# First feed-forward stage with four plain columns, weight splits held until the norm factor's chain is emitted, rotary tables on GpSimd in the second feed-forward stage

## The chip, the cores and the metric

The kernel runs on one core of one Trainium2 chip. The metric is the device time of one execution in microseconds (us); the number for a kernel is the median of several runs. Engines are named as in the profile: PE (TensorE matmuls), PEld (its weight loads), DVE (VectorE), ACT (ScalarE), POOL (GpSimd) and SP (SyncE, which issues the DMAs).

## The reference

A trunk of two layers in fp32 on 512 tokens of width 1024. Each layer is a half-step SwiGLU feed-forward (width 2816), an attention, and a second half-step feed-forward; all of them behind an RMS norm.

```python
def rms_norm(x, gain):
    y = xf * lax.rsqrt(jnp.mean(xf * xf, axis=-1, keepdims=True) + EPS)
    return (y * gain.astype(jnp.float32)).astype(x.dtype)

def swiglu(h, w_gate_up, w_down):
    gate, up = jnp.split(h @ w_gate_up, 2, axis=-1)
    return (jax.nn.silu(gate) * up) @ w_down

def rope_angles(positions):
    inv_freq = ROPE_THETA ** (-jnp.arange(0, ROT_DIM, 2, dtype=jnp.float32) / ROT_DIM)
    ang = positions.astype(jnp.float32)[..., None] * inv_freq
    return jnp.cos(ang), jnp.sin(ang)

for i in range(DEPTH):
    x = x + 0.5 * swiglu(rms_norm(x, norm_gains[i, 0]), ffn_w_gate_up[i, 0], ffn_w_down[i, 0])
    h = rms_norm(x, norm_gains[i, 1])
    # i = 0: stick-breaking attention; i = 1: sliding-window attention, which uses the rotary tables
    x = x + attention(h)
    x = x + 0.5 * swiglu(rms_norm(x, norm_gains[i, 2]), ffn_w_gate_up[i, 1], ffn_w_down[i, 1])
```

## The kernel before, in words

**Stages.** The kernel runs six stages in the order "0", "s", "1", "2", "w", "3". "0" to "3" are the feed-forwards, "s" the stick-breaking and "w" the sliding-window attention. x is kept in SBUF with features on the partitions, as eight tiles of 128x512 (`x[k]`). Each fp32 product is made of three matmuls: x and the weights are split into a high part (a rounding to fp32r) and a low part (what is left), and hi·hi, hi·lo and lo·hi are added. ACT casts the high part of a weight (L345), DVE subtracts for the low part (L350, in `_split`); the lines read L85 where an engine wrapper keeps program order.

**A feed-forward stage.** Its 22 hidden columns of 128 are made in two ways. The first three (`PLAIN`) are plain columns: two units each (gate and up), each unit eight k-tiles of three matmuls of 128x512, into one PSUM bank of 512 columns. The others are "seven" columns (`seven`, L528): a Strassen-like scheme with seven products of four k-tiles of three matmuls of 128x256. Their partial sums live in banks named a (tag "tr", two buffers), b (tag "pv", one) and c (tag "z", one). The down projection (`down`, L631) runs over groups of columns (`GROUPS`: 3, 3, 4, 4, 4, 4); its pieces for a group are put between the seven columns of the next group. A piece needs the `hs` of all columns of its group.

**The norm factor.** Matmuls run on x times the gain, not on the normed x; the factor 1/rms is multiplied in afterwards. `norm_tile` (L423) makes xh, xl and adds the squares into `acc`. `norm_rows` (L453) sums `acc` on PE (ss, tag "pv") and runs a chain of twelve dependent small DVE steps (nv, nr, nt). `norm_bcast` (L463) spreads the factor over the partitions (dg on ACT, bc on PE, `rbc`). `swiglu` (L486) multiplies gate and up by `rbc` (g and h on DVE, silu on ACT) and `keep` splits the result into `hs` (cast on ACT, rest on DVE). `sums_of_x` (L497) makes t0 to t3, the sums of x that the seven columns need.

**The plain part** (`plain`, L596). Units 0 to 2 use the banks of tag "mm" (three), unit 3 uses tag "z", units 4 and 5 tag "mm" again. So unit 4 takes the bank of unit 0, which is free when swiglu(0) has read it. In stage "0" the first three units run interleaved over the k-tiles. Behind the last k-tile of unit 1 (in stage "0" behind the fifth k-tile of unit 3) stand `norm_bcast`, `sums_of_x((2, 3))` and `swiglu(0)`, in this order.

**What sets the order.** A scheduler orders the instructions of each engine when the program is built; after that each engine works strictly in that order and waits for semaphores. PE always keeps the order of the code, DVE does in `plain` only (`self.order(True)`). `pump` (L289) loads and splits weights as far ahead as the rings allow: raw tiles (3, in feed-forwards 2 more), split slots (3 and 2 more) and half slots (2). SP issues the loads in the order of the code.

**The rotary tables** (`rope_tables`, L886). Some 45 dependent steps on 128x32 elements (an argument reduction and two Sin lookups on ACT) make cos and sin, which stage "w" uses. They are emitted in the output projection of stage "s", behind n = 3 (`project_out`, L819), and run on DVE.

Of the kernel before, what the change touches and what calls it, by code (L numbers as in the profile page):

```python
# [15 lines left out]
P = 128  # L16
# [10 lines left out]

PLAIN = 3
GROUPS = (3, 3, 4, 4, 4, 4)
MORE_RAWS, MORE_SLOTS, HALF_SLOTS = 2, 2, 2  # L30
# [104 lines left out]

def ffn_steps():

    steps = [("plain", u) for u in range(2 * PLAIN)]
    f, last = PLAIN, None
    for g, size in enumerate(GROUPS):  # L140
        ends = sum(GROUPS[: g + 1])
# [18 lines left out]
    return steps + [("down", len(GROUPS) - 1, n) for n in range(KD)]  # L160


def ffn_slots(steps):

    slots, units = [], []

    def slot(name, raws):
        if name not in slots:
            slots.append(name)
            units.extend(r for r in raws if r not in units)  # L170

    for step in steps:
        if step[0] == "plain":
            slot(step, [step])
        elif step[0] == "seven":
            _, p, f = step
            slot(*{
                1: (("A22 A11", f), [("g", f), ("u", f)]), 4: (("A22 A11", f), []), 5: (("S1 S3", f), []), 7: (("S1 S3", f), []),
                2: (("A12", f), []), 6: (("S2 S4", f), []), 3: (("S2 S4", f), []),
            }[p])  # L180
        else:
            _, g, n = step
            for i in range(n * GROUPS[g], (n + 1) * GROUPS[g]):
                slot(("d", g, i // KD), [("d", g, i // KD)])
    return slots, units


class _Trunk:
    def __init__(self, tc, pools, psum, aps):
# [10 lines left out]
        self.half_rings = []  # L200
        self.fp = self.stage = None
        self.roped = False

# [37 lines left out]
    def queue_ffn(self, st):  # L241

        steps = ffn_steps()
        slots, units = ffn_slots(steps)
        raw = {u: len(self.loads) + i for i, u in enumerate(units)}
# [12 lines left out]
        for step in steps:  # L258
# [7 lines left out]
            else:  # L266
                _, g, n = step
                tiles = [(at["d", g, i // KD], i % KD) for i in range(n * GROUPS[g], (n + 1) * GROUPS[g])]
            out.append((step, tiles))
# [19 lines left out]
    def pump(self):  # L289

        moved = True
        while moved:
# [275 lines left out]

    def ffn(self, st, steps, following, first=False):
        tc, nc = self.tc, self.nc  # L570
        with tc.tile_pool(name="ffn", bufs=1) as fp:
# [4 lines left out]
            self.cells, self.hs = {}, {}  # L576
            self.plain(steps[: 2 * PLAIN], first)
            last = len(GROUPS) - 1
            tail = [s for s in steps if s[0][:2] == ("down", last)]
            for step, tiles in steps[2 * PLAIN : len(steps) - len(tail)]:  # L580
# [15 lines left out]
    def plain(self, steps, first):  # L596

        xs = list(zip(self.xh, self.xl))
        banks, self.ts = {}, []
        units = range(2 * PLAIN)  # L600
        order = [(k, u) for u in units for k in range(KD)]
# [3 lines left out]
        rows, cast = ((1, KD - 1), (3, 4)) if first else ((0, KD - 1), (1, KD - 1))  # L605
        self.order(True)
        self.pump()
        for k, u in order:
            if u not in banks:
                banks[u] = self.psum.tile([P, T], F32, tag="z", name="gu", bufs=1) if u == UNITS else self.bank("gu")  # L610
            wh, wl, used = self.tile(*steps[u][1][k])
            self.mm3(banks[u], [((wh, wl), xs[k])], first=(k == 0), last=(k == KD - 1))
            if (u, k) == rows:
                self.norm_rows()
            self.used(*used)
# [10 lines left out]
    def down_terms(self, ps, g, tiles, at):  # L626
        f0 = sum(GROUPS[:g])
        for j, (n, i) in enumerate(tiles, at):
            self.mm3(ps, [(self.tile(n, i), self.hs[f0 + j])], first=(j == 0), last=(j == GROUPS[g] - 1))

    def down(self, n, g, tiles, following, ps=None):  # L631
        at = GROUPS[g] - 1 if ps is not None else 0
# [186 lines left out]
    def project_out(self, parts, opened, following):  # L819
        for n in range(KD):  # L820
# [3 lines left out]
            following(n)  # L824
            if n == UNITS and not self.roped:
                self.rope_tables()

# [58 lines left out]
    def rope_tables(self):  # L886
# [6 lines left out]
        with self.tc.tile_pool(name="rope", bufs=1) as rp:  # L893
            V = nc.vector

# [12 lines left out]
            part = _split_const(two_pi, 12, 3)  # L908
            q, t = tile_("q"), tile_("t")

# [4 lines left out]
            def fma(a, k, cst):  # L915
                V.scalar_tensor_tensor(a, k, cst, a, ALU.mult, ALU.add)

# [12 lines left out]
            for d, rest in digits:  # L930
                for m, piece in enumerate(_split_const(rest, 12, 3)):
                    if m == 0:
                        V.tensor_scalar(t, d, piece, None, ALU.mult)
# [280 lines left out]
def build(tc, aps, stages="0s12w3"):  # L1214
    from contextlib import ExitStack

    with ExitStack() as ctx:
# [27 lines left out]
        for i, st in enumerate(stages):  # L1245
# [5 lines left out]
            if st in "0123":  # L1251
                net.ffn(st, steps[st], following, first=(i == 0))
            else:
# [3 lines left out]
def layout(x, positions, norm_gains, ffn_w_gate_up, ffn_w_down, sb_w_in, sb_w_out,  # L1257
# [7 lines left out]
    for i in range(4):  # L1265
        units = []
        for name in ffn_slots(ffn_steps())[1]:
            if name[0] == "plain":
# [5 lines left out]
            else:  # L1274
                _, g, m = name
                f, size = sum(GROUPS[:g]), GROUPS[g]
                tiles = dn[i, :, f : f + size].reshape(KD * size, P, P)[m * KD : (m + 1) * KD]
# [33 lines left out]
```

## Time and profile before

| what | us |
|---|---|
| three runs | 1879.17, 1881.69, 1884.75 |
| median | 1881.69 |
| the profiled execution | 1884.44 |
| its span, first to last instruction | 1882.6 |
| PE busy | 1834.2 |
| DVE busy | 1500.1 |
| ACT busy | 938.1 |
| POOL busy | 170.2 |

The mean granted TensorE clock of the profiled execution is 0.985 of full speed. Rows of the trace are read so: a chain row has the start, the duration and what ran ("44.22 0.61 DVE g L85"); a timeline row has start, duration, engine, line, operation, out<-in, shapes, and in brackets the idle time before it and what ended that; a row of waits has who waited for whom, the total, how many times, and the longest. In a group of matmuls "a x12" are the twelve of one product.

### The profile page before, as it was taken

To read this page: it belongs to the slowest core of one execution; us is meant where nothing else is said; L and a number is where in the kernel's file an instruction comes from. 1 tells how busy PE (TensorE), PEld (TensorE's weight loads), DVE (VectorE), ACT (ScalarE), POOL (GpSimd) and SP (SyncE) were. 2 spreads that over 40 slices of the span, in tenths; PEclk is the share of its full clock that TensorE was granted. 3 is DMA by queue.
4 is the path that set the end of the run, shared out by engine and by line. 5 is a ranking of instruction groups with operands and counts; after the bars stand their busy time and mean duration, and the time that the engine had idled before them with its cause. 6 is when DMAs were issued, how large, how long until landed. Compare 5 with 4: busy or idle time off the path is not lost.

```text
span 1882.6 us, 29285 instructions
## 1 busy us (share of the span) xinstructions
PE 1834.2 (97%) x11730; PEld 1651.1 (88%) x11730; DVE 1500.1 (80%) x2426; ACT 938.1 (50%) x1497; POOL 170.2 (9%) x131
## 2 busy tenths in 40 slices
PE   7999999999999999999999999999999899999999
PEld 5999999878787789999988999999887788999998
DVE  8888888668886988878768888787678588888884
ACT  6444444465664644444446444444356564444441
POOL 1000000333230100000010000000242210000000
PEclk8999999999999999999999999999989899999999
DMA  4333333221121423333323323322211043233331
GB/s 168 101 101 101 101 104 99 69 78 57 57 68 34 134 83 98 105 109 97 106 68 123 101 90 105 119 88 92 73 58 33 12 134 101 95 108 101 102 101 57
DMA packets 48809, 170.95 MB, mean 91 GB/s; under 512 B 5792, under 2 KB 6048, under 8 KB 48672
## 3 DMA queue, kind: packets, MB, share of 16 engines
q1 hardware_dynamic: 48672, 169.07, 28.2%
q8 instruction: 92, 1.51, 0.3%
q14 instruction: 45, 0.37, 0.1%
HBM read 166.96 MB, written 2.10 MB: 90 GB/s over the span
## 4 chain that ended last, share of the span: by engine, by line
PE 80%; DVE 11%; ACT 4%; issue 3%; POOL 1%; DMA 0%; SPq 0%; ACTq 0%; DVEq 0%; POOLq 0%
PE dn L85 25%; PE a L85 23%; PE c L85 11%; PE b L85 6%; PE gu L85 4%; PE tok L85 3%; PE op L85 3%; DVE keep L732 2%; PE pv L85 1%; DVE beta L733 1%; DVE t L85 1%; DVE qs L645 1%; PE sc L85 1%; DVE wt L755 1%; ACT keep L726 1%
## 5 line engine op out<-in xcount | busy, mean ns | idle before, releaser
L85 PE MATMUL dn<-hs,slot 128*128 128x512 f32 x1152 | 279.1, 391 | 0.0
L85 PEld LDWEIGHTS dn<-hs,slot 128*128 128x128 f32 x1152 | 211.0, 188 | 40.4
L85 PE MATMUL dn<-hs,slotx 128*128 128x512 f32 x960 | 234.2, 392 | 2.2 <-DVE hs L85 1.3
L345 ACT CAST slot<-raw 128x1024 fp32r<-128x1024 f32 (+1 forms) x155 | 160.0, 1033 | 145.1 <-PE a L85 55.2
L85 PE MATMUL a<-t,slot 128*128 128x256 f32 x1728 | 230.2, 283 | 0.0
L85 PEld LDWEIGHTS a<-t,slot 128*128 128x128 f32 x1728 | 222.7, 191 | 6.6
L85 PEld LDWEIGHTS dn<-hs,slotx 128*128 128x128 f32 x960 | 175.4, 188 | 37.5 <-DVE hs L85 2.2
L474 DVE SCALAR_TENSOR_TENSOR x<-dn,x 128x512 f32<-128x512 f32 x192 | 131.5, 685 | 44.9 <-PE dn L85 44.8
L350 DVE TENSOR_TENSOR slot<-raw,slot 128x1024 fp32r<-128x1024 f32 (+1 forms) x117 | 143.8, 1231 | 9.9 <-ACT slot L345 9.9
L85 PEld LDWEIGHTS a<-t,slotx 128*128 128x128 f32 x1008 | 131.0, 191 | 5.3
L85 PE MATMUL a<-t,slotx 128*128 128x256 f32 x1008 | 134.1, 283 | 0.0
L348 POOL TENSOR_TENSOR slot<-raw,slot 128x512 fp32r<-128x512 f32 x60 | 87.6, 1485 | 477.4 <-ACT slot L345 473.4
L85 PE MATMUL b<-xh,half 128*128 128x256 f32 x608 | 121.8, 283 | 0.0
L441 POOL TENSOR_TENSOR acc<-acc,sq 128x512 f32<-128x512 f32 x30 | 44.3, 1476 | 804.3 <-ACT sq L440 804.3
L85 PE MATMUL tok<-slot,xh 128*128 128x256 f32 x576 | 113.6, 296 | 0.1
L85 PEld LDWEIGHTS b<-xh,half 128*128 128x128 f32 x608 | 100.3, 192 | 0.0
L345 ACT CAST slotx<-raw 128x1024 fp32r<-128x1024 f32 x64 | 66.8, 1050 | 66.4 <-PE a L85 56.7
L345 ACT CAST slot<-rawx 128x1024 fp32r<-128x1024 f32 x60 | 63.1, 1052 | 69.7 <-PE a L85 43.6
L85 PE MATMUL c<-xh,slot 128*128 128x256 f32 x480 | 96.2, 283 | 0.0
L85 PEld LDWEIGHTS tok<-slot,xh 128*128 128x128 f32 x576 | 92.2, 197 | 3.3 <-issue 1.3
L553 DVE TENSOR_TENSOR g<-c,r 128x256 f32<-128x256 f32 x76 | 32.2, 424 | 75.8 <-PE c L85 75.6
L85 PE MATMUL gu<-xh,slot 128*128 128x512 f32 x256 | 87.3, 412 | 3.8 <-ACT xh L432 1.7
(360 smaller groups left out, 4216.7 us busy)
## 6 DMA issues: line engine op xcount, KB each, us to landing
raw<-in_w_dram SPq DMA_DIRECT2D x165, 512.0 KB, 3.5
rawx<-in_w_dram SPq DMA_DIRECT2D x96, 512.0 KB, 3.5
raw<-in_sbqk_dram SPq DMA_DIRECT2D x16, 512.0 KB, 3.4
raw<-in_swin_dram SPq DMA_DIRECT2D x10, 512.0 KB, 3.5
raw<-in_sbv_dram SPq DMA_DIRECT2D x8, 512.0 KB, 3.4
raw<-in_sbo_dram SPq DMA_DIRECT2D x8, 512.0 KB, 3.4
raw<-in_swo_dram SPq DMA_DIRECT2D x8, 512.0 KB, 3.4
x<-in_xt_dram SPq DMA_DIRECT2D x8, 256.0 KB, 5.4
```

Source lines behind the costliest of these rows:

```text
L85: return self._tc.keep_in_program_order(method(*args, **kwargs))
L345: nc.scalar.copy(hi, src)
L348: nc.gpsimd.tensor_sub(lo[:, h], src[:, h], hi[:, h])
L350: nc.vector.tensor_sub(lo, src, hi)
L441: (nc.gpsimd if k < POOL_SQUARES else nc.vector).tensor_add(self.acc, self.acc, sq)
L474: self.nc.vector.scalar_tensor_tensor(self.x[n], ps, factor, self.x[n], ALU.mult, ALU.add)
L553: nc.vector.tensor_add(g[:, W2:], ps, self.cells["r6", f])
L645: nc.vector.tensor_sub(out[other, h, :], src[own, :], out[own, h, :])
L726: nc.scalar.activation(keep[:, :, :n], z[:, :, :n], AF.Sigmoid, scale=-0.125)
L732: nc.vector.tensor_tensor_scan(rev, rev, rev, 1.0, ALU.mult, ALU.bypass)
L733: nc.vector.tensor_mul(beta[:, :, : n - 1], beta[:, :, : n - 1], keep[:, :, 1:n])
L755: nc.vector.tensor_sub(lo, src, hi)
```

## The change

It does four things. (1) `PLAIN` and `GROUPS` become tables by stage: stage "0" has four plain columns and a first group of four; the other stages keep three. (2) In stage "0" nothing is split by `pump` from the start of `plain` until `norm_rows` has been emitted (`hold`). (3) In all four feed-forwards unit 4 takes the bank of tag "pv" instead of one of tag "mm", and `swiglu(0)` is emitted ahead of `sums_of_x((2, 3))`. (4) The rotary tables are emitted in stage "1", behind the last product of column 11, and run on GpSimd; a fused multiply-add on DVE becomes two instructions there. Two of the steps, the clamp and the absolute value, stay on DVE.

```diff
-PLAIN = 3
-GROUPS = (3, 3, 4, 4, 4, 4)
+PLAIN = {"0": 4, "1": 3, "2": 3, "3": 3}
+GROUPS = {st: (4, 3, 3, 4, 4, 4) if st == "0" else (3, 3, 4, 4, 4, 4) for st in PLAIN}
...
-            if n < len(self.plan) and not self.plan[n][5] and max(self.plan[n][2]) < len(self.raws) and self._open():
+            if n < len(self.plan) and not self.hold and not self.plan[n][5] and max(self.plan[n][2]) < len(self.raws) and self._open():
...
                 if step[0] == "seven":
                     self.seven(step[1], step[2], tiles)
+                    if angles and step[1:] == (7, NF // 2):
+                        self.rope_tables()
...
         self.order(True)
+
+        self.hold = first
         self.pump()
         for k, u in order:
             if u not in banks:
-                banks[u] = self.psum.tile([P, T], F32, tag="z", name="gu", bufs=1) if u == UNITS else self.bank("gu")
+                tag = {UNITS: "z", UNITS + 1: "pv"}.get(u)
+                banks[u] = self.psum.tile([P, T], F32, tag=tag, name="gu", bufs=1) if tag else self.bank("gu")
...
             if (u, k) == rows:
                 self.norm_rows()
+                self.hold = False
             self.used(*used)
             if (u, k) == rows:
                 self.sums_of_x((0, 1))
             if (u, k) == cast:
                 self.norm_bcast()
+                self.swiglu(0, (banks[0], banks[1]))
                 self.sums_of_x((2, 3))
-                self.swiglu(0, (banks[0], banks[1]))
...
             following(n)
-            if n == UNITS and not self.roped:
-                self.rope_tables()
...
-            V = nc.vector
+            V = nc.gpsimd
...
             def fma(a, k, cst):
-                V.scalar_tensor_tensor(a, k, cst, a, ALU.mult, ALU.add)
+                V.tensor_scalar(m, k, cst, None, ALU.mult)
+                V.tensor_add(a, a, m)
...
-            V.tensor_scalar(ang, ang, PI_LOW, -PI_LOW, ALU.min, ALU.max)
-            V.scalar_tensor_tensor(t, ang, -1.0, ang, ALU.mult, ALU.max)
+            nc.vector.tensor_scalar(ang, ang, PI_LOW, -PI_LOW, ALU.min, ALU.max)
+            nc.vector.scalar_tensor_tensor(t, ang, -1.0, ang, ALU.mult, ALU.max)
```

Three places show how the order of the instructions moves. The first is DVE in stage "0", around the first step of the norm chain (nv); slot and slotx are split weights. Before:

```order
L441 TENSOR_TENSOR acc_132<-acc_132,sq_198 128x512 [waits Activation_49]
L441 TENSOR_TENSOR acc_132<-acc_132,sq_206 128x512 [waits Activation_49]
L85 TENSOR_TENSOR slotx3_236<-raw3_209,slotx3_236 128x1024 [waits DMAHW0_49,Activation_49]
L85 TENSOR_TENSOR slotx4_241<-raw4_211,slotx4_241 128x1024 [waits DMAHW1_49,Activation_49]
L85 TENSOR_TENSOR slot5_299<-raw5_213,slot5_299 128x1024 [waits DMAHW2_49,Activation_49]
L85 TENSOR_SCALAR nv_119<-ss_316 128x4 [waits PE_49]
L85 TENSOR_SCALAR nr_120<-nv_119 128x4 [waits DVE_49]
L85 TENSOR_SCALAR nr_120<-nr_120 128x4 [waits DVE_49]
```

And after the change:

```order
L443 TENSOR_TENSOR acc_132<-acc_132,sq_198 128x512 [waits Activation_49]
L443 TENSOR_TENSOR acc_132<-acc_132,sq_206 128x512 [waits Activation_49]
L85 TENSOR_SCALAR nv_119<-ss_301 128x4 [waits PE_49]
L85 TENSOR_SCALAR nr_120<-nv_119 128x4 [waits DVE_49]
L85 TENSOR_SCALAR nr_120<-nr_120 128x4 [waits DVE_49]
...
L85 SCALAR_TENSOR_TENSOR nr_120<-nt_121,nr_120 128x4 [waits DVE_49]
L85 TENSOR_TENSOR slotx3_318<-raw3_209,slotx3_318 128x1024 [waits DMAHW0_49,Activation_49]
L85 TENSOR_TENSOR slotx4_323<-raw4_211,slotx4_323 128x1024 [waits DMAHW1_49,Activation_49]
L85 TENSOR_TENSOR slot5_328<-raw5_213,slot5_328 128x1024 [waits DMAHW2_49,Activation_49]
L85 TENSOR_TENSOR slot6_333<-rawx6_234,slot6_333 128x1024 [waits DMAHW7_49,Activation_49]
```

The three splits that stood ahead of nv now stand behind the last step of its chain (nr).

The second is DVE in the plain part of stage "1", around swiglu(0) (g, h, hs0). Before:

```order
L85 TENSOR_TENSOR g_6401<-gu_6273,rbc_6377 128x512
L85 SCALAR_TENSOR_TENSOR h_6402<-gu_6342,rbc_6377 128x512
L85 TENSOR_TENSOR h_6402<-g_6401,h_6402 128x512 [waits DVE_49,Activation_49]
L85 TENSOR_TENSOR hs0_6407<-h_6402,hs0_6407 128x512 [waits Activation_49]
L85 TENSOR_TENSOR sums_6436<-rawx104_6259,rawx105_6264 128x1024 [waits DMAHW5_49]
L85 TENSOR_TENSOR slot143_6435<-sums_6436,slot143_6435 128x1024 [waits Activation_49]
```

And after:

```order
L85 TENSOR_TENSOR g_6258<-gu_6152,rbc_6256 128x512 [waits Activation_49]
L85 SCALAR_TENSOR_TENSOR h_6259<-gu_6221,rbc_6256 128x512
L948 TENSOR_SCALAR ang_7792<-ang_7792 128x32 [waits Pool_49]
L949 SCALAR_TENSOR_TENSOR t_7802<-ang_7792 128x32 [waits DVE_49]
L85 TENSOR_TENSOR h_6259<-g_6258,h_6259 128x512 [waits Activation_49]
L85 TENSOR_TENSOR hs0_6264<-h_6259,hs0_6264 128x512 [waits Activation_49]
L85 TENSOR_TENSOR t_6270<-xg_6267 128x256 [waits Activation_49] x2
L85 SCALAR_TENSOR_TENSOR t_6270<-t_6270,xg_6267 128x256 [waits DVE_49] x2
```

The clamp (L948 in the changed kernel) and the absolute value (L949) of the rotary tables now stand between swiglu(0)'s h and its next step, and the clamp waits for POOL. The sums for t2 and t3 (t rows) follow.

The third is PE at the first seven column of stage "1", where the product c ends and b begins. Before:

```order
L85 MATMUL c_6570<-t2_6387,slot143_6435 128x256 x3
L85 MATMUL c_6570<-t3_6397,slot143_6435 128x256 x3
L85 MATMUL b_6585<-xh1_5996,half144_6440 128x256 [waits PE_49]
L85 MATMUL b_6585<-xl1_5997,half144_6440 128x256
L85 MATMUL b_6585<-xh1_5996,half144_6440 128x256
```

And after:

```order
L85 MATMUL c_6449<-t2_6275,slot141_6314 128x256 x3
L85 MATMUL c_6449<-t3_6285,slot141_6314 128x256 x3
L85 MATMUL b_6464<-xh1_5939,half142_6319 128x256 [waits DVE_49]
L85 MATMUL b_6464<-xl1_5940,half142_6319 128x256
L85 MATMUL b_6464<-xh1_5939,half142_6319 128x256
```

b's first matmul now waits for DVE, which reads the bank "pv" in swiglu(2), where before it waited for a matmul.

The steps of the tables themselves are 61 instructions on POOL ahead of the clamp: a cast and eight multiplications on 128x4, and 52 on 128x32. SP issues the load of the positions behind two raw loads of stage "1", where before it stood in stage "0".

More of the change, by code (lines that the diff above doesn't have):

```diff
@@ L133, in take, with ffn_steps @@
         return self.pool.tile(shape, dtype, tag=self.tag, name=f"{self.tag}{n}", bufs=self.bufs)
[L136 to L141, printed above, removed]
+def ffn_steps(st):
+    groups = GROUPS[st]
+    steps = [("plain", u) for u in range(2 * PLAIN[st])]
+    f, last = PLAIN[st], None
+    for g, size in enumerate(groups):
+        ends = sum(groups[: g + 1])
         pieces = [("down", g - 1, n) for n in range(KD)] if g else []
@@ L159, in ffn_steps, with ffn_slots @@
     assert last is None
-    return steps + [("down", len(GROUPS) - 1, n) for n in range(KD)]
-def ffn_slots(steps):
+    return steps + [("down", len(groups) - 1, n) for n in range(KD)]
+def ffn_slots(st, steps):
     slots, units = [], []
@@ L182, in ffn_slots @@
             _, g, n = step
-            for i in range(n * GROUPS[g], (n + 1) * GROUPS[g]):
+            for i in range(n * GROUPS[st][g], (n + 1) * GROUPS[st][g]):
                 slot(("d", g, i // KD), [("d", g, i // KD)])
@@ L241, in queue_ffn @@
     def queue_ffn(self, st):
-        steps = ffn_steps()
-        slots, units = ffn_slots(steps)
+        steps = ffn_steps(st)
+        slots, units = ffn_slots(st, steps)
         raw = {u: len(self.loads) + i for i, u in enumerate(units)}
@@ L567, in seven, with ffn @@
         self.used(n, HALF)
-    def ffn(self, st, steps, following, first=False):
+    def ffn(self, st, steps, following, first=False, angles=False):
         tc, nc = self.tc, self.nc
@@ L576, in ffn @@
             self.cells, self.hs = {}, {}
-            self.plain(steps[: 2 * PLAIN], first)
-            last = len(GROUPS) - 1
+            head = 2 * PLAIN[st]
+            self.plain(steps[:head], first)
+            last = len(GROUPS[st]) - 1
             tail = [s for s in steps if s[0][:2] == ("down", last)]
-            for step, tiles in steps[2 * PLAIN : len(steps) - len(tail)]:
+            for step, tiles in steps[head : len(steps) - len(tail)]:
                 if step[0] == "seven":
                     self.seven(step[1], step[2], tiles)
+                    if angles and step[1:] == (7, NF // 2):
+                        self.rope_tables()
                 else:
@@ L599, in plain @@
         banks, self.ts = {}, []
-        units = range(2 * PLAIN)
+        units = range(len(steps))
         order = [(k, u) for u in units for k in range(KD)]
@@ L614, in plain @@
                 self.norm_rows()
+                self.hold = False
             self.used(*used)
@@ L626, in down_terms @@
     def down_terms(self, ps, g, tiles, at):
-        f0 = sum(GROUPS[:g])
+        groups = GROUPS[self.stage]
+        f0 = sum(groups[:g])
         for j, (n, i) in enumerate(tiles, at):
-            self.mm3(ps, [(self.tile(n, i), self.hs[f0 + j])], first=(j == 0), last=(j == GROUPS[g] - 1))
+            self.mm3(ps, [(self.tile(n, i), self.hs[f0 + j])], first=(j == 0), last=(j == groups[g] - 1))
     def down(self, n, g, tiles, following, ps=None):
-        at = GROUPS[g] - 1 if ps is not None else 0
+        at = GROUPS[self.stage][g] - 1 if ps is not None else 0
         ps = self.bank("dn") if ps is None else ps
@@ L930, in rope_tables @@
             for d, rest in digits:
-                for m, piece in enumerate(_split_const(rest, 12, 3)):
-                    if m == 0:
+                for j, piece in enumerate(_split_const(rest, 12, 3)):
+                    if j == 0:
                         V.tensor_scalar(t, d, piece, None, ALU.mult)
@@ L1251, in build @@
             if st in "0123":
-                net.ffn(st, steps[st], following, first=(i == 0))
+                net.ffn(st, steps[st], following, first=(i == 0), angles=(st == "1"))
             else:
@@ L1275, in layout @@
                 _, g, m = name
-                f, size = sum(GROUPS[:g]), GROUPS[g]
+                f, size = sum(GROUPS[st][:g]), GROUPS[st][g]
                 tiles = dn[i, :, f : f + size].reshape(KD * size, P, P)[m * KD : (m + 1) * KD]
```

7 lines of the change are left out of this document (4 added, 3 removed).

## The prediction

> **What bounds the kernel now.** I read the head of the page first: the busy shares of the engines, then the first line of the chain that ended last.
>
> ```profile
> span 1882.6 us, 29285 instructions
> ...
> PE 1834.2 (97%) x11730; PEld 1651.1 (88%) x11730; DVE 1500.1 (80%) x2426; ACT 938.1 (50%) x1497; POOL 170.2 (9%) x131
> ...
> PE 80%; DVE 11%; ACT 4%; issue 3%; POOL 1%; DMA 0%; SPq 0%; ACTq 0%; DVEq 0%; POOLq 0%
> ```
>
> TensorE (PE) is busy for 97% of the span and carries 80% of the chain. The change leaves the matmuls almost as they are, so what can move is PE's idle time and its clock. The waits of PE show which idle time the change can reach (total, times, longest):
>
> ```profile
> PE gu L85 <- DVE g L85: 10.8, 1, 10.8
> ...
> PE gu L85 <- ACT xh L432: 1.7, 1, 1.7
> ...
> PE dn L85 <- DVE hs L85: 1.3, 3, 0.8
> ...
> PE dn L85 <- ACT hs L482: 0.9, 3, 0.3
> ...
> PE gu L85 <- DVE xl L433: 0.5, 1, 0.5
> ```
>
> The 10.8 us are in stage "0": its fifth plain unit needs a PSUM bank that `swiglu(0)` frees with g. The chain over that window shows where the wait ends:
>
> ```profile
> 44.22 0.61 DVE g L85
> 44.87 13.84 PE gu L85 x48
> 58.72 1.43 PE a L85 x12
> ```
>
> The timelines of PE and of VectorE (DVE) show why g was late:
>
> ```profile
> 23.84 0.95 PE L85 MATMUL ss<-ones,acc 128*128 128x1 f32 x8
> ```
>
> ```profile
> 22.58 2.36 DVE L85 TENSOR_TENSOR slotx<-raw,slotx 128x1024 fp32r<-128x1024 f32 x2 [0.25 <-ACT slotx L345]
> 24.86 1.22 DVE L85 TENSOR_TENSOR slot<-raw,slot 128x1024 fp32r<-128x1024 f32 x1
> 25.99 0.15 DVE L85 TENSOR_SCALAR nv<-ss 128x4 f32<-128x4 f32 x1
> ```
>
> Three weight splits stand ahead of the norm chain's first step, nv. After the stall 48 matmuls take 13.84 us. At full speed 24 of them take 5.44 (the stage "2" row below), so 48 take 10.9; the other 2.9 us went to the clock. How the clock answers to idle time is seen in a table by stretches around the second gap, at the start of stage "1" (busy time of PE, PEld, DVE, ACT, POOL, then the granted clock):
>
> ```profile
> 640.96:644.38 3.42, 1.21 (x5) 0.48 (x3) 3.25 (x5) 3.00 (x5) 0.00 (x0) 1.00 0.90 347
> 644.38:647.79 3.41, 3.41 (x13) 2.97 (x14) 3.28 (x7) 2.95 (x5) 0.00 (x0) 0.51 0.86 308
> 647.79:651.20 3.41, 3.41 (x10) 2.64 (x9) 3.16 (x12) 2.81 (x6) 0.00 (x0) 0.50 0.76 255
> ```
>
> A stretch with 1.21 of 3.42 us busy is followed by 6.8 us at half clock, which loses 3.4 us of work. I price each new PE gap of some 3 us at 1.7 to 3.4 us more (one half-clock stretch or two), 2.6 in the middle.
>
> The Trainium skill's page "TensorE: Matmul & The Clock Gate", section "HAM oscillation", puts the rule as no PE-idle gap over about 3.4 us. This trace is stricter, since gaps of 1.7 and 0.5 us within one stretch cost half the clock behind them. By the page's rule the sum would come out without the four terms of 2.6, which is rival 4.
>
> **Stage "0".** The splits move behind the norm chain, swiglu(0) moves ahead of `sums_of_x((2, 3))`, and unit 4 goes to the "pv" bank, so it waits for nothing. nv can start once the sum of squares is there, at 24.8. The four plain columns then run through, with at most a short wait for a late split. Gained: 10.8 of wait and 2.9 of clock, 13.7. Lost: a plain column is 48 x 0.227 = 10.9 us, a seven column 84 x 0.119 = 10.0 (12 of its matmuls in 1.43), so 0.9. Net −12.8 before new waits.
>
> Two new waits follow. First, b of the first seven column also lives in the "pv" bank and now needs swiglu(2)'s g, which reads unit 4. In stage "2", below, that is worth 3.2 us; here two more units lie between, so I take 1.0 (bounds 0 and 3.2). Second, the first down piece needs four hs instead of three. Before, the last plain unit ended at 58.72 and hs2 was finished 5.9 us later, by the DVE timeline; the chain has the down piece:
>
> ```profile
> 63.94 0.69 DVE L85 TENSOR_TENSOR hs<-h,hs 128x512 fp32r<-128x512 f32 x1 [0.35 <-ACT hs L482]
> ```
>
> ```profile
> 65.91 2.07 PE dn L85 x9
> ```
>
> PE reached the end of the third term 9.3 us after that unit; with the 1.0 it reaches the fourth at 10.3. In DVE's queue two splits of 1.14 and one more swiglu of four steps of 0.6 now stand in the same stretch: 5.9 + 1.0 + 2.3 + 2.4 = 11.6, so hs3 is 1.3 late by DVE alone. On ScalarE (ACT) its cast stands behind a weight cast and a copy that wait for PE, which can double that; I take 3 (bounds 0 and 5), and 2.6 for the clock. Stage "0": −12.8 + 1.0 + 3 + 2.6 = **−6.2**.
>
> **Stage "1", the rotary tables leave DVE.** Before, they ran among the residuals of the output projection and held back the last residual and with it xh. The chain's rows, and PE's timeline, at the starts of stages "1", "2" and "3":
>
> ```profile
> 677.24 1.43 PE a L85 x12
> ```
>
> ```profile
> 990.29 5.44 PE gu L85 x24
> ```
>
> ```profile
> 1530.66 5.44 PE gu L85 x24
> ```
>
> ```profile
> 636.65 0.39 PE L85 MATMUL gu<-xh,slot 128*128 128x512 f32 x1
> ```
>
> ```profile
> 1024.63 0.28 PE L85 MATMUL a<-xh,slot 128*128 128x256 f32 x1
> ...
> 1027.51 0.28 PE L85 MATMUL b<-xh,half 128*128 128x256 f32 x1
> ```
>
> ```profile
> 1565.00 0.28 PE L85 MATMUL a<-xh,slot 128*128 128x256 f32 x1
> ...
> 1567.87 0.28 PE L85 MATMUL b<-xh,half 128*128 128x256 f32 x1
> ```
>
> From the first plain matmul, S, to the first seven matmul, a, it is 677.24 − 636.65 = 40.6 us in stage "1" and 34.3 in the two others. So −6.2 when the tables are gone.
>
> **Stages "1" to "3", the pv bank.** b comes 2.9 us behind the first a, and now waits for swiglu(2)'s g; DVE's timeline in stages "2" and "3":
>
> ```profile
> 1030.02 0.68 DVE L85 TENSOR_TENSOR g<-gu,rbc 128x512 f32<-128x512 f32 x1
> ```
>
> ```profile
> 1570.44 0.68 DVE L85 TENSOR_TENSOR g<-gu,rbc 128x512 f32<-128x512 f32 x1
> ```
>
> In stage "2" g ended at 1030.70 where b took its bank at 1027.51: 3.2 us. In stage "3" 1571.12 − 1567.87 = 3.25. The swap of swiglu(0) with the sums changes the order ahead of this g, not the amount of work, so I leave g where it is. Given back is the wait for hs at the first down piece: 1.3 + 0.9 = 2.2 us over six places by the waits above, of which I count 0.7 a stage. With the clock, 3.2 − 0.7 + 2.6 = **+5.1 in each of stages "2" and "3"**. Bounds: 0 if g comes sooner; 7 with two half-clock stretches and the down wait kept.
>
> **Stage "1", the tables on GpSimd (POOL).** DVE's clamp (L948) stands between swiglu(0)'s second and third step and waits for POOL's whole chain. Behind it queue hs0, the sums for t2 and t3, the column's S1/S3 weights, swiglu(1) and swiglu(2). PE then waits for the z bank (c, freed by swiglu(1)'s h) and for the pv bank (b).
>
> When the chain starts: its position DMA is issued behind raw loads that wait for the splits ahead of the norm. DVE's timeline has those splits for stage "2", the page's last part the DMA, the groups by line the nearest POOL rows:
>
> ```profile
> 993.83 2.35 DVE L85 TENSOR_TENSOR slotx<-raw,slotx 128x1024 fp32r<-128x1024 f32 x2
> ```
>
> ```profile
> pos<-in_pos_dram SPq DMA_DIRECT2D x1, 2.0 KB, 4.7
> line<-in_sinks_dram SPq DMA_DIRECT2D x1, 8.0 KB, 1.8
> ```
>
> ```profile
> L961 POOL TENSOR_TENSOR q<-ra,rb 128x256 f32<-128x256 f32 x3 | 2.2, 739 | 0.2
> ...
> L960 POOL TENSOR_TENSOR rb<-q,sin 128x128 f32<-128x128 f32 x3 | 1.4, 464 | 0.0
> ...
> L1300 POOL MEMSET const-float32-1.0<- 128x1 f32 x1 | 0.1, 99 | 0.0
> ```
>
> The splits end at 996.18, S + 5.9; a DMA of this size lands 1.8 to 4.7 later; the chain starts at S + 8 to S + 11, I take 9. No POOL arithmetic on 32 elements is in the trace. 739 ns at 256 and 464 at 128 give 0.26 us at 32 on a line, an estimate; the one-element memset, 0.10, bounds it below, the 128-element row above. The chain has 52 instructions on 32 elements and nine on four, nearly all waiting for the one before, which adds 0.07 (0.2 us of idle over the three of L961). 52 x 0.33 + 9 x 0.15 = 18.5. Bounds: 10 near the memset, 25 at 0.46 a step. Its end: S + 27.5, from S + 18 to S + 36.
>
> When DVE reaches the clamp, by its timeline in stage "2":
>
> ```profile
> 1006.50 0.75 DVE L85 TENSOR_TENSOR t<-xg 128x256 f32<-128x256 f32 x2
> ...
> 1011.77 0.68 DVE L85 TENSOR_TENSOR g<-gu,rbc 128x512 f32<-128x512 f32 x1
> ...
> 1023.61 0.68 DVE L85 SCALAR_TENSOR_TENSOR h<-gu,rbc 128x512 f32<-128x512 f32 x1
> ```
>
> The sums for t2 and t3, 1006.50 to 1011.77, now follow. So g starts at S + 16.2 and the clamp is reached near S + 17.8. DVE stands some 10 us (0 to 18). Swiglu(1)'s h, which ended at 1024.29 = S + 34.0, then ends at S + 43, with an estimated 1 us of DVE's idle time taken up; c wants its bank at S + 35.8: 7.2. b then waits for g, S + 40.4 + 9 = 49.4, against c's end at 44.5: 4.9. Together 12.1; plus 2.6 of clock, less 0.7 at the down piece, less the 6.2: stage "1" **+7.8**. With no wait at the clamp it is −6.2 + 5.1 = −1.1, with 18 us about +16.
>
> **Sum.** −6.2 + 7.8 + 5.1 + 5.1 = +11.8 on the profiled execution (1884.44 us: the span and 1.8 around it). That execution lies 2.75 over the median of the three runs, 1881.69. Forecast: 1881.7 + 11.8 = **1893.5**.
>
> **Rivals.** (1) *The pv bank costs nothing and the clamp finds the tables done: faster.* If DVE and ACT deliver swiglu(2)'s g before b's turn, and POOL is over by S + 18, what is left is −6.2 − 6.2 = −12.4: **1869**, or 1874 with one of the pv gaps left. It decides at a POOL step under 0.2 us and a g that comes 3.2 us sooner. For it: the order ahead of g does change; against: DVE is busy for 80% of the span, and the amount of work ahead of g doesn't shrink. Chance 0.2. (2) *POOL in time, pv bank as counted*: −6.2 − 1.1 + 5.1 + 5.1 = +2.9, **1884.6**, no change. Chance 0.13. (3) *POOL slow*, 25 us: stage "1" +16, sum +20, **1902**. Chance 0.15. (4) *The new gaps cost no clock*, because each is split over two stretches that stay mostly busy: +11.8 − 4 x 2.6 = +1.4, **1883**. For it: the gaps are of 3 to 5 us at a random place in the stretches; against: 2.2 us of idle time were enough before. Chance 0.1. (5) *The hold only moves stage "0"'s wait* to a split that now comes late: stage "0" near 0 and the sum +18, 1900, inside the range. The forecast itself, with (5), has 0.42.
>
> **Numbers.** About 0.3%, 5.6 us, is what a measurement of this kernel can tell from no change. Slower by more: the forecast and rival 3, with a little of 2: 0.6. Same: the rest of rival 2 and rival 4: 0.2. Faster: 0.2. The range leaves out the far part of rival 1 and the end of rival 3: 1874 to 1907. The forecast's own range is 1887 to 1901.
>
> **What would show it.** Right: no wait of gu on g in stage "0"; in stage "1" DVE waits some 10 us for POOL at the clamp, c and b wait for DVE, half clock follows; in stages "2" and "3" b waits for DVE some 3 us. Wrong: POOL steps under 0.2 us and the clamp passed at once; b without a gap; gaps of 3 us at full clock.

## The result and the profile after

| | us |
|---|---|
| before, median of 4 runs (1879.17 to 1884.92) | 1883.22 |
| after, median of 4 runs (1901.30 to 1906.42) | 1903.74 |
| ratio, with its 95% interval | 1.0129 (1.0107 to 1.0151) |
| profiled execution after, its span | 1901.3, 1899.5 |

The change makes the kernel slower by 1.3%. The ratio isn't the quotient of the two medians, which is 1.0109. It agrees with the 18 runs of the kernel before that the first four experiments are compared with (median 1879.43 us; 1903.74 / 1879.43 = 1.0129). By the ratio the change costs some 24 us, by the two medians of the table 20.5, by the two profiled executions 16.9 (1901.3 − 1884.44): the profiled execution of after is the lowest of its four, that of before one of the highest of its kernel. Of stage times and rows below, differences are between profiled executions; of kernels, they are ratios, each against the runs of the kernel before that are listed with it.

The head of the page after: PE is busy for 1.1 us less than before in a span that is 16.9 us longer, so its idle time grew, from 48.4 us to 66.4.

```profile
span 1899.5 us, 29209 instructions
...
PE 1833.1 (97%) x11694; PEld 1650.1 (87%) x11694; DVE 1488.0 (78%) x2371; ACT 933.1 (49%) x1491; POOL 191.0 (10%) x195
```

The waits of PE after. The 10.8 us of gu for g are gone, as are the waits for xh and xl; two new rows lead the list:

```profile
PE c L85 <- ACT g L494: 16.2, 1, 16.2
PE b L85 <- DVE g L85: 15.0, 4, 4.6
...
PE dn L85 <- ACT hs L484: 2.0, 1, 2.0
...
PE dn L85 <- DVE hs L85: 0.9, 1, 0.9
```

The waits of DVE name the cause of the first, and DVE's timeline shows its place in the plain part of stage "1":

```profile
DVE ang L948 <- POOL ang L925: 17.0, 1, 17.0
```

```profile
645.96 0.68 DVE L85 TENSOR_TENSOR g<-gu,rbc 128x512 f32<-128x512 f32 x1
646.55 0.68 DVE L85 SCALAR_TENSOR_TENSOR h<-gu,rbc 128x512 f32<-128x512 f32 x1
664.22 0.18 DVE L948 TENSOR_SCALAR ang<-ang 128x32 f32<-128x32 f32 x1 [16.99 <-POOL ang L925]
```

DVE is done with the second step of swiglu(0) at 647.2 and then does nothing for 17 us, until POOL's chain is over. (The row of c names ACT's silu, which ended at 681.50; DVE's h, which frees the bank of c, ended at 681.43. Both stand behind the clamp.) POOL's timeline, with its first and last steps:

```profile
640.60 0.46 POOL L910 CAST posf<-pos 128x4 f32<-128x4 int32 x1 [17.86 <-DMA pos<-in_pos_dram]
641.14 5.27 POOL L914 TENSOR_SCALAR ang<-posf 128x4 f32<-128x4 f32 x8
646.49 0.22 POOL L920 TENSOR_SCALAR d<-ang 128x32 f32<-128x32 f32 x1
646.79 0.30 POOL L921 TENSOR_SCALAR d<-d 128x32 f32<-128x32 f32 x1
...
663.93 0.25 POOL L925 TENSOR_TENSOR ang<-ang,m 128x32 f32<-128x32 f32 x1
```

And what PE made of it, from its timeline (S, the first plain matmul, then the first seven column):

```profile
629.29 0.39 PE L85 MATMUL gu<-xh,slot 128*128 128x512 f32 x1
...
663.79 0.28 PE L85 MATMUL a<-xh,slot 128*128 128x256 f32 x1
...
681.59 2.90 PE L85 MATMUL c<-t,slot 128*128 128x256 f32 x12 [16.20 <-ACT g L494]
689.06 0.58 PE L85 MATMUL b<-xh,half 128*128 128x256 f32 x1 [4.58 <-DVE g L85]
```

The plain part of stage "1" is 34.5 us long now (40.4 before), then PE stands for 16.2 and 4.6 us, and c runs at half speed (12 matmuls in 2.9 us instead of 1.44). The clock by stretches:

```profile
664.80:668.20 3.40, 0.58 (x5) 0.38 (x4) 2.30 (x6) 2.86 (x6) 0.97 (x3) 1.00 0.00 0
668.20:671.60 3.40, 0.00 (x0) 0.00 (x0) 3.37 (x7) 2.43 (x3) 0.00 (x0) 0.86 0.00 0
...
681.90:685.30 3.40, 2.59 (x12) 2.29 (x11) 2.48 (x4) 1.16 (x3) 0.00 (x0) 0.50 0.30 117
...
688.70:692.10 3.40, 3.04 (x14) 3.04 (x15) 2.72 (x6) 1.25 (x2) 0.00 (x0) 0.50 0.80 273
692.10:695.50 3.40, 3.40 (x21) 3.40 (x21) 1.11 (x3) 0.99 (x2) 0.00 (x0) 0.64 0.02 7
```

Stage by stage, from the first matmul of one stage to that of the next in PE's timeline, the two executions differ by −4.8 us in "0", −2.5 in "s", +17.9 in "1", +4.4 in "2", −2.6 in "w" and +4.6 in "3"; that is the whole 16.9. The four stages that the forecast covers add up to +22.1. In "s" and "w" PE's idle time is nearly the same (10.3 us and 9.4, 15.6 and 14.2), the rest of their 5.1 us is a higher granted clock (0.987 and 0.993, 0.938 and 0.946); in the twelve other profiles below these two stages differ from before by −1.0 to −2.6 and by −0.2 to −5.9, whatever was changed.

### The profile page after: what moved, and what is told of

Same layout as the page of the kernel before. It is cut to its first block, busy times and chain, and to the rows that moved or that the text cites. A ratio compares the mean times of both kernels' runs of the same rounds, so it can differ in the third digit from the quotient of the medians.

```text
span 1899.5 us, 29209 instructions
## 1 busy us (share of the span) xinstructions
PE 1833.1 (97%) x11694; PEld 1650.1 (87%) x11694; DVE 1488.0 (78%) x2371; ACT 933.1 (49%) x1491; POOL 191.0 (10%) x195
## 4 chain that ended last, share of the span: by engine, by line
PE 77%; DVE 12%; ACT 4%; issue 3%; POOL 2%; DMA 1%; SPq 0%; ACTq 0%; DVEq 0%; POOLq 0%
PE dn L85 24%; PE a L85 22%; PE c L85 11%; PE b L85 6%; PE op L85 4%; PE tok L85 3%; PE gu L85 3%; DVE keep L742 2%; DVE beta L743 1%; PE pv L85 1%; DVE t L85 1%; DVE qs L655 1%; PE sc L85 1%; DVE wt L765 1%; ACT slot L347 1%
## 5 line engine op out<-in xcount | busy, mean ns | idle before, releaser
L352 DVE TENSOR_TENSOR slot<-raw,slot 128x1024 fp32r<-128x1024 f32 (+1 forms) x117 | 144.8, 1239 | 10.8 <-ACT slot L347 10.7
L85 PE MATMUL gu<-xh,slot 128*128 128x512 f32 x288 | 94.7, 401 | 2.1 <-ACT slot L347 1.7
```

The costliest lines, as they stand in the source:

```text
L85: return self._tc.keep_in_program_order(method(*args, **kwargs))
L352: nc.vector.tensor_sub(lo, src, hi)
```

## The experiments

Theory A: the clamp's wait on POOL, with all of stage "1" queued behind it on DVE, is the larger part of the loss. Rival, theory B: the four waits of b for the "pv" bank and the half clock behind them are the larger part.

**The clamp out of the plain part.** The chain on POOL stays as it is; only the place of two DVE instructions moves, behind column 11.

```diff
-            nc.vector.tensor_scalar(ang, ang, PI_LOW, -PI_LOW, ALU.min, ALU.max)
-            nc.vector.scalar_tensor_tensor(t, ang, -1.0, ang, ALU.mult, ALU.max)
+            nc.ordered.tensor_scalar(ang, ang, PI_LOW, -PI_LOW, ALU.min, ALU.max)
+            nc.ordered.scalar_tensor_tensor(t, ang, -1.0, ang, ALU.mult, ALU.max)
```

> The clamp and the absolute value of the rotary tables keep program order on DVE, behind the last product of column 11, instead of standing in the plain part of stage "1"; everything else is the changed kernel. Theory A (the clamp's wait on GpSimd, 17.0 us, with all of stage "1" queued behind it on DVE, is the larger part of the loss): no DVE wait on POOL over 1 us, c of the first seven column of stage "1" starts without a gap, stage "1" some 19 us shorter, 1903.7 - 19 = 1885 us, near the kernel before. Theory B (the four waits of b for the bank "pv", 15.0 us, with the half clock behind them, are the larger part, and the clamp's wait is mostly covered): 1903.7 - 7 = 1897 us. Both expect b of stage "1" to wait 3.5 to 4.6 us.

Measured: 1885.97 us, 1.0034 (1.0020 to 1.0047) of before. c starts without a gap, b still waits, and stage "1" takes 353.8 us instead of 371.4. From 1.0129 to 1.0034 is some 18 us: theory A.

**The "pv" bank in stage "0" only.**

```diff
-                tag = {UNITS: "z", UNITS + 1: "pv"}.get(u)
+                tag = {UNITS: "z", UNITS + 1: "pv" if first else None}.get(u)
```

> Unit 4 takes the bank "pv" in stage "0" only; stages "1" to "3" use a bank of tag "mm" as the kernel before. The clamp stays where the changed kernel has it. Theory A: the clamp still waits 17 us and c of stage "1" some 16; only b's waits of stages "1" to "3" go (4.6, 3.7, 4.6), with about 2 us of clock each in stages "2" and "3", less about 1 us each for the first down piece: 1903.7 - 13 = 1891 us. Theory B: 1903.7 - 20 = 1884 us.

Measured: 1897.13 us, 1.0091 (1.0073 to 1.0109): some 7 us gained, not 13, and far from theory B's 20. b of the later stages waits no more, but the first down piece of stages "1" and "3" now does (the next run shows it).

**Both edits together.**

> Both edits of the two kernels before together. If the two costs are separate and add up, stage "0" keeps its gain of 4.8 us, the start of stage "1" its 5.9, and stages "2" and "3" are as before: 1883.2 - 10.7 = 1872.5 us, by theory A and B alike. If what the rows show as waits is only moved (the norm chain or the down pieces become late instead), it stays at 1880 or above.

Measured: 1879.46 us, 0.9998 (0.9983 to 1.0013). The two costs add up (18 + 7 of 24), and yet the gain that the two profiled executions promised, 4.8 us in stage "0" and 5.9 at the start of stage "1", isn't there. PE's timeline in stage "3" of this kernel, and of the kernel before, at the first down piece:

```profile
1569.49 0.50 PE L85 MATMUL dn<-hs,slotx 128*128 128x512 f32 x1 [1.71 <-ACT hs L484]
1571.18 1.22 PE L85 MATMUL dn<-hs,slotx 128*128 128x512 f32 x2 [1.19 <-DVE hs L85]
```

```profile
1574.05 0.50 PE L85 MATMUL dn<-hs,slotx 128*128 128x512 f32 x1 [0.32 <-ACT hs L482]
1575.40 0.72 PE L85 MATMUL dn<-hs,slotx 128*128 128x512 f32 x2 [0.84 <-DVE hs L85]
```

Where b's wait is gone, hs2 is late: 2.9 us instead of 1.2, and the stage's granted clock is 0.990 instead of 1.000. DVE's g of swiglu(2) ends 42.1 us behind the stage's first matmul instead of 40.6, and ACT's timeline shows the rest. A weight cast that waits for the product c stands ahead of the silu of the last plain column, where before the silu came first:

```profile
1566.48 1.05 ACT L347 CAST slotx<-raw 128x1024 fp32r<-128x1024 f32 x1 [1.11 <-PE c L85]
1567.43 0.63 ACT L494 ACTIVATE g<-g 128x512 f32<-128x512 f32 x1
1568.82 0.62 ACT L484 CAST hs<-h 128x512 fp32r<-128x512 f32 x1 [0.76 <-DVE h L85]
```

```profile
1571.22 0.64 ACT L492 ACTIVATE g<-g 128x512 f32<-128x512 f32 x1
1572.44 1.05 ACT L345 CAST slotx<-raw 128x1024 fp32r<-128x1024 f32 x1 [0.58 <-PE c L85]
1573.39 0.61 ACT L482 CAST hs<-h 128x512 fp32r<-128x512 f32 x1
```

**The tables back on DVE**, in the output projection, the rest as in the changed kernel (the diff is the pieces of (4), reversed).

> The rotary tables as in the kernel before (on DVE, in the output projection of stage "s"); the rest is the changed kernel. Theory A: stage "0" -4.8, the start of stage "1" as slow as before (40.4 us from its first plain to its first seven matmul), b's waits +4 to +5 in each of stages "1" to "3": 1883.2 - 4.8 + 13.5 = 1892 us. Theory B: little is gained by it, 1898 us or above.

Measured: 1891.23 us, 1.0060 (1.0041 to 1.0079), as theory A has it. So moving the tables to POOL cost 0.7% of the time as it was done, though it took 5.9 us off the start of stage "1".

**The swap in stage "0" only**, on top of the two edits. Theory C: the swap of swiglu(0) with the sums reorders ACT so that hs2 is late. Rival, theory D: something that stays does it.

```diff
                 self.norm_bcast()
-                self.swiglu(0, (banks[0], banks[1]))
+                if first:
+                    self.swiglu(0, (banks[0], banks[1]))
                 self.sums_of_x((2, 3))
+                if not first:
+                    self.swiglu(0, (banks[0], banks[1]))
```

> The kernel with the clamp in program order and the bank "pv" in stage "0" only, with one more edit: swiglu(0) stands ahead of the sums (2, 3) in stage "0" only, and behind them in stages "1" to "3" as in the kernel before. Theory C (the swap makes hs2's cast on ACT late in stages "1" and "3", where PE now waits 3.0 and 2.9 us at the first down piece against 0.5 and 1.2 before, and loses clock behind it): those waits go back, stage "1" -2.5 and stage "3" -4.6 us: 1879.5 - 7 = 1872.5 us. Theory D (the late down piece comes from something else that stays, the tables' place or the fourth plain column): 1879.5 us, the same waits.

Measured: 1872.86 us, 0.9963 (0.9949 to 0.9977), faster than both kernels: theory C.

**The first group of stage "0" back to three.**

```diff
-GROUPS = {st: (4, 3, 3, 4, 4, 4) if st == "0" else (3, 3, 4, 4, 4, 4) for st in PLAIN}
+GROUPS = {st: (3, 4, 4, 4, 4, 3) if st == "0" else (3, 3, 4, 4, 4, 4) for st in PLAIN}
```

> As the run before it, and stage "0" has the groups (3, 4, 4, 4, 4, 3) instead of (4, 3, 3, 4, 4, 4), so its first down piece needs three hs, while four columns stay plain. Theory C: the waits of 2.05 and 0.92 us for hs3 in stage "0" and the half clock behind them go: 1872.5 - 5 = 1867.5 us. If the down piece waits for hs2 just as long, nothing is gained: 1872.5 us.

Measured: 1869.90 us, 0.9946 (0.9928 to 0.9964). The wait for hs3 is gone; the difference to the run before, 0.0017, is not beyond the two intervals.

**Stage "0" alone**: the four plain columns, the hold, the "pv" bank and the swap in stage "0", all else as before.

> Stage "0" as in the changed kernel (four plain columns, hold, bank "pv", swiglu(0) ahead of the sums), everything else as before: tables on DVE in the output projection, the mm bank and the old order in stages "1" to "3". By the rows of the profiled executions stage "0" gains 2 to 5 us: 1879.4 - 3.5 = 1876 us. If the 10.8 us of wait that the change removes come back whole at b and at the first down piece, 1879.4 us or above.

Measured: 1877.67 us, 0.9988 (0.9973 to 1.0003). A gain of 2 us that its interval doesn't set apart from none.

**The angles laid out contiguously**, on the changed kernel, to price the eight multiplications, which took 5.27 us, 0.66 each in the mean:

```diff
-            a3 = ang.rearrange("p (b f) -> p b f", b=TB)
+            a3 = ang.rearrange("p (f b) -> p b f", b=TB)
```

(and t3 likewise)

> The changed kernel with the angles laid out frequency by frequency, so that each of the eight first multiplications on GpSimd writes four neighbouring elements instead of four that lie 32 bytes apart. In the changed kernel these eight took 5.27 us. If the stride is the cause they take 2 us or less, the clamp's wait falls from 17.0 to about 13.7 and the time by as much, 1903.7 - 3.3 = 1900 us. If an instruction on four elements costs 0.66 whatever its layout, nothing changes.

Measured: 1905.20 us, 1.0135 (1.0103 to 1.0168). The eight take 5.32 us; the stride isn't the cause.

**The same eight on 32 down to 4 elements**, laid out as in the run before.

```diff
+            wide = tile_("wide")
+            w3 = wide.rearrange("p (f b) -> p f b", b=TB)
+            V.tensor_copy(w3, pf[:, None, :].broadcast_to([P, NROT, TB]))
             for f in range(NROT):
-                V.tensor_scalar(a3[:, :, f], pf, INV_FREQ[f], None, ALU.mult)
+                V.tensor_scalar(ang[:, f * TB :], wide[:, f * TB :], INV_FREQ[f], None, ALU.mult)
```

> The changed kernel, with the positions first copied out to 32 elements and the eight multiplications by the frequencies made on 32, 28, 24, 20, 16, 12, 8 and 4 elements, each overwriting the tail of the one before. It gives GpSimd's price by size. If few elements are dear in themselves (0.66 us on four, 0.22 to 0.30 on 32 in the changed kernel), the first take about 0.3 and the last ones 0.6; the eight and the copy come to some 3.5 us instead of 5.3, and the clamp waits about 15 us. If the price is fixed by this kind of instruction, all take 0.66 and nothing moves. Either way the time stays within 3 us of the changed kernel's.

Measured: 1902.71 us, 1.0141 (1.0112 to 1.0171). POOL's timeline:

```profile
643.71 0.29 POOL L915 COPY wide<-posf 128x32 f32<-128x32 f32 x1
644.09 5.28 POOL L917 TENSOR_SCALAR ang<-wide 128x32 f32<-128x32 f32 x8
```

Again 5.3 us for the eight, but not 0.66 each. The groups by shape show three that take over 1 us and one on four elements that takes 0.22 (the last column is idle time):

```profile
L917 POOL TENSOR_SCALAR ang<-wide 128x24 f32<-128x24 f32 x1 | 1.1, 1052 | 0.1
L917 POOL TENSOR_SCALAR ang<-wide 128x20 f32<-128x20 f32 x1 | 0.3, 258 | 0.1
L917 POOL TENSOR_SCALAR ang<-wide 128x4 f32<-128x4 f32 x1 | 0.2, 224 | 0.1
```

The long ones (24, 16 and 12 elements) lie beside DVE's three 128x1024 subtractions of that stretch. In the changed kernel, where all eight have four elements, they take 0.22 to 1.28 us. So neither of the two answers that the expectation offers is right: it is neither the size nor the kind of instruction. The timeline of the kernel with the clamp in order shows the same over the whole chain; there DVE works on while POOL's chain runs. POOL first, then DVE:

```profile
657.21 1.03 POOL L925 TENSOR_TENSOR ang<-ang,m 128x32 f32<-128x32 f32 x1
658.31 1.09 POOL L920 TENSOR_SCALAR q<-t 128x32 f32<-128x32 f32 x1
...
665.68 0.25 POOL L925 TENSOR_TENSOR ang<-ang,m 128x32 f32<-128x32 f32 x1
...
666.32 1.14 POOL L924 TENSOR_SCALAR m<-d 128x32 f32<-128x32 f32 x1
667.53 0.29 POOL L921 TENSOR_SCALAR q<-q 128x32 f32<-128x32 f32 x1
...
668.50 1.25 POOL L925 TENSOR_TENSOR t<-t,m 128x32 f32<-128x32 f32 x1
```

```profile
656.90 2.43 DVE L85 TENSOR_TENSOR t<-t,t 128x1024 fp32r<-128x1024 f32 x2
...
666.07 1.24 DVE L85 TENSOR_TENSOR slotx<-rawx,slotx 128x1024 fp32r<-128x1024 f32 x1 [1.20 <-ACT slotx L347]
667.23 0.68 DVE L85 TENSOR_TENSOR g<-gu,rbc 128x512 f32<-128x512 f32 x1
...
668.43 1.21 DVE L338 TENSOR_TENSOR sums<-raw,rawx 128x1024 f32<-128x1024 f32 x1
```

A POOL step that starts while DVE runs an instruction with two inputs in SBUF lasts until some 0.1 us after that instruction ends (1.14 beside the slotx split, 1.25 beside the sums); beside g, whose first input is in PSUM, or with DVE idle, it takes 0.25 to 0.29.

**The best kernel without the hold** (`self.hold = False` in place of `self.hold = first`).

> The best kernel so far (clamp in order, bank "pv" and swap in stage "0" only, groups (3, 4, 4, 4, 4, 3) there, 1869.9 us) without the hold: three splits stand ahead of the norm chain again. The chain then starts 1.2 us later (25.99 against 24.8 in the first profile), and the first swiglu with it; with unit 4 in the bank "pv" PE has no wait that hangs on that before b. Expected 0 to 3 us slower, 1870 to 1873 us.

Measured: 1865.55 us, 0.9939 (0.9920 to 0.9958), the fastest of all, where 0 to 3 us of loss were expected; but it lies within the interval of the kernel with the hold. The hold brings nothing that can be told, and DVE's timelines say why. With the hold (the changed kernel), then without it:

```profile
24.86 0.16 DVE L85 TENSOR_SCALAR nv<-ss 128x4 f32<-128x4 f32 x1 [2.38 <-PE ss L85]
...
38.97 0.69 DVE L85 TENSOR_TENSOR g<-gu,rbc 128x512 f32<-128x512 f32 x1
```

```profile
22.37 2.36 DVE L85 TENSOR_TENSOR slotx<-raw,slotx 128x1024 fp32r<-128x1024 f32 x2 [0.25 <-ACT slotx L347]
24.64 1.22 DVE L85 TENSOR_TENSOR slot<-raw,slot 128x1024 fp32r<-128x1024 f32 x1
25.89 0.17 DVE L85 TENSOR_SCALAR nv<-ss 128x4 f32<-128x4 f32 x1
...
36.96 0.68 DVE L85 TENSOR_TENSOR g<-gu,rbc 128x512 f32<-128x512 f32 x1
```

nv comes 1.0 us sooner with the hold, but DVE has stood idle for 2.4 us to get it, and the three splits still have to be made, now ahead of swiglu(0). So its g comes 2.0 us later with the hold than without it. The kernel of the run with the first group of three, which differs by the hold alone, has its g at 39.61, 2.7 us later; there b waits 2.1 us for the "pv" bank, and without the hold it doesn't wait.

**The best kernel without the "pv" bank in stage "0"** (tag "z" for unit 3 alone, all others "mm").

> The best kernel so far with unit 4 of stage "0" in a bank of tag "mm", as the kernel before. Unit 4 then waits for swiglu(0)'s second step, which ends at about 40 us, where PE is ready for it at about 34: a wait of 5 to 6 us in place of b's 2.1, and some half clock: 3 to 6 us slower, 1873 to 1876 us. If the hold and the swap alone bring swiglu(0) early enough, it stays at 1870.

Measured: 1878.56 us, 1.0004 (0.9991 to 1.0017). PE's timeline has unit 4 waiting for g, and one more unit later:

```profile
40.52 0.80 PE L85 MATMUL gu<-xh,slotx 128*128 128x512 f32 x1 [5.12 <-DVE g L85]
...
62.13 0.52 PE L85 MATMUL gu<-xh,slot 128*128 128x512 f32 x1 [2.72 <-DVE g L85]
```

In stage "0" the bank is worth 7.7 us by the profiles (380.2 us against 372.5 with it) and some 11 by the ratios (1.0004 against 0.9946), more than the 3 to 6 expected. Without it the stage takes 2.6 us longer than in the kernel before, although the first wait has fallen from 10.8 us to 5.1.

**The positions loaded early**, with the clamp in order (the load emitted ahead of stage "s", into a tile that lasts).

> The kernel with the clamp in program order (1886 us), and the positions loaded ahead of stage "s". Nothing waits for the tables there, so the time stays as it was; the look is for the start of GpSimd's chain. In the changed kernel its first instruction started 11.3 us behind the first plain matmul of stage "1", released by the load. If the load alone holds it, it now starts before that matmul, right behind GpSimd's last addition of squares.

A single run, which allows no verdict on the time: 1886.39 us. POOL's timeline:

```profile
634.83 0.19 POOL L913 CAST posf<-pos 128x4 f32<-128x4 int32 x1 [6.79 <-PE op L85]
```

It starts 0.2 us behind the first plain matmul (634.60) instead of 11.3, not ahead of it as expected: what releases it is now the last matmul of stage "s". So the late load held the chain back by 11 us.

## Why the prediction was wrong in size, point by point

The direction and the place were right: slower, by the clamp's wait in stage "1" and by b's waits for the "pv" bank. The forecast was +11.8 us, 1893.5; measured are +16.9 by the profiled executions, +20.5 by the medians and some +24 by the ratio. The median, 1903.74 us, lies inside the wide range and outside the forecast's own, 1887 to 1901. The step that failed is the term of stage "1", the tables on POOL.

- **The tables on POOL: here it failed.** DVE reached the clamp at S + 17.9 (17.8 forecast), but POOL's chain ended at S + 34.9, not S + 27.5. Its start was S + 11.3 instead of 9: the load was issued at S + 6.5 and took 4.7 us, which I had only as an upper end. The nine instructions ahead of the 52 took 5.9 with their gaps, not 1.35. I priced four elements below 32, but the shortest took 0.22 us and up to the next 0.08, as on 32; that makes some 2.7, and the rest is DVE's work beside them. The 52 steps took 17.7 us (17.2), so the line through 256 and 128 elements held; it held because DVE stood still beside them. DVE stood 17.0 us instead of 10, and c waited 16.2 instead of 7.2: none of DVE's idle time was there to take up. The term of stage "1" was +17.9 instead of +7.8, twice the error of 5.1 on the profiled executions. That error is as small as it is by luck, since "s" and "w", which the sum has at nothing, came out 5.1 us shorter.
- **Stage "0"**, −6.2 forecast, −4.8 in the profile. No wait of gu on g is left, b waits 2.1 us (1.0 taken), the first down piece 2.9 (3 taken), and a later column 1.0 for a weight split (not in the sum). The kernel with this part alone gains only 2.1 us by the medians, and the nine other profiles with the same stage "0" show −1.1 to −3.7, so −4.8 is more than the part is worth on average. The prediction blames the splits ahead of nv for the late g. They held nv back by some 1 us; in the kernel before, the chain is over at 28.3 and g starts at 44.13, with the sums for t2 and t3 and the splits of the first seven column in between. The runs show the gain coming from the bank, and the hold making swiglu(0) later. Rival 5 had seen that the hold could fail, though not in this way.
- **Tables off DVE**, −6.2 forecast; the start of stage "1" went from 40.4 us to 34.5, −5.9. The forecast took the ends of its 40.6 and 34.3 from two different views.
- **The pv bank in stages "2" and "3"**, +5.1 each; +4.4 and +4.6. That these come so close is luck: b waits 3.7 and 4.6 us instead of 3.2, and the clock takes about 1.2 each by the difference, not 2.6.
- **What I had as rival 3** (a slow POOL, 1902 us, chance 0.15) is what happened, by another way than its price of 0.46 a step. The prediction says that by the rule it quotes all four terms of 2.6 fall away (rival 4), but the gap that it forecasts for c, 7.2 us, is longer than that rule's limit, so only three of the four could have gone.
- **What I missed:** the swap isn't neutral in stages "1" to "3". I left g of swiglu(2) where it was, but it ends 0.6 us later in stage "2" and 1.4 in "3", which is what b waits more than forecast; and on ACT a silu now stands behind a cast that waits for PE. In the changed kernel this is hidden by b's wait; it is worth 0.35% (0.9998 to 0.9963) once that is gone.

The sum of the parts closes on the ratio's 24 us in two ways. By stages it is −2.1 for stage "0" (the run of it alone) and +17.9, +4.4 and +4.6 for the others: 24.8. By kernels it is 18 us for the clamp, 7 for the pv bank in three stages, 7 for the swap in two of them once the other is gone, against a gain of 7 us (0.9963) by the tables off DVE's path and stage "0". Open is how the gain in stage "0" splits between clock and waits: the stage took 372.8 us in the changed kernel and 375.5 in the one with contiguous angles, with nearly the same idle time (9.0 and 9.2).

## What to carry to other kernels

A short chain moved to an idle engine isn't free if one of its steps comes back to a busy, in-order engine: look where that step stands in the queue, and compare the chain's end with the time that the queue gets there. Here moving two tiny instructions by some 180 places was worth 18 us, more than any other part of the change cost or won. And a borrowed buffer pays only where it takes a wait away: the same "pv" bank is worth some 8 to 11 us in stage "0" and makes PE wait 3.7 to 4.6 us in each stage that had no such wait.

## What the runs showed of the hardware

- A POOL instruction on 32 elements takes 0.22 to 0.30 us and the next dependent one starts some 0.08 later; beside a DVE instruction with two SBUF inputs it lasts until that one has ended, up to 1.26 us. The chain that took 23.6 us with DVE standing still for the last 17 of them (640.60 to 664.18) took 34.9 in the kernel where DVE worked on (644.74 to 679.62). The Trainium skill's page "SBUF — State Buffer", section "Who interferes with whom", says that a DVE instruction with two SBUF inputs contends with a GpSimd instruction that reads SBUF; the rows agree, including that g, with one input in PSUM, doesn't.
- By the differences of stage times and idle times, a gap of PE of 3.7 us cost 1.2 us of clock, one of 16.2 and one of 4.6 together some 3.5. Two waits of 1.71 and 1.19 us in stage "3" cost 2.8 in the kernel with both edits (356.7 us against 352.1 before, of which 1.7 is added idle time) and 1.5 in the one with the "pv" edit alone (355.3); two of 1.75 and 1.28 in stage "1" of the former cost nearly nothing (350.1 us against 348.2 with the swap undone, of which 1.9 is idle time). So the length of a gap alone doesn't set what it costs. That it depends on how the gap lies in the clock's stretches is a guess that no run here tests.
